# A buffer of its own for the convolution beside a recurrence, and scheduler priorities for the recurrence

## The chip, the cores and the metric

The kernel runs on one core of a Trainium2 chip. The metric is the device time of one execution in microseconds (us). Five engines work side by side, each through a queue of its own: TensorE (PE in the profile, with its weight loads as PEld), VectorE (DVE), ScalarE (ACT), GpSimd (POOL) and SyncE (SP), which here issues the transfers.

## The reference, cut to what matters

Two layers of a hybrid backbone over 768 tokens (256 of context, 512 latent), width 2048. In each layer one input projection feeds four groups of heads: a gating MLP, differential attention, a bidirectional recurrence (RWKV-7) and a short gated convolution. The recurrence and the convolution are the two that matter here:

```python
def rwkv_scan(r, k, v, decay, kk, a, s0):
    def step(S, inp):
        r_t, k_t, v_t, w_t, kk_t, a_t = inp
        sa = jnp.einsum('bhvk,bhk->bhv', S, -kk_t)
        S = (S * w_t[:, :, None, :] + sa[..., None] * (kk_t * a_t)[:, :, None, :]
             + v_t[..., None] * k_t[:, :, None, :])
        y = jnp.einsum('bhvk,bhk->bhv', S, r_t)
        return S, y

def short_conv(bg, cg, xin, w):
    z = cg * xin
    y = lax.conv_general_dilated(z, w[:, None, :].astype(z.dtype), window_strides=(1,),
                                 padding=[(CONV_W // 2, CONV_W // 2)], ...)
    return bg * y
```

The scan runs once forwards and once backwards over the context and then over the latent tokens; the two results are added, normalised by head and gated. All groups are gated, joined and sent through an output projection. The second layer needs no context outputs.

## The kernel before

**Main products.** A main product is a tile of 128 output features of a projection over all tokens (`mtile`). Each float32 weight tile is split into a high part `wh` (ACT, L276) and a low part `wl` (three of four on POOL, the rest on DVE, L277), and for each of the 16 blocks of 128 inputs three matmuls (L306) add high and low terms into PSUM: 48 matmuls of 512 columns for the latent tokens, and 48 of 256 for the context where it is wanted. The results rotate through three PSUM banks of the pool `mm`. A bank comes free when ACT or DVE has copied or used its result (`evac`, L331 and L333; `gate2`, L344 and L345).

**The recurrence.** It is cut into segments of 256 tokens: per layer 4 feature tiles (`ft`) times 3 parts times 2 directions, 24 segments, 48 in all. `rwkv_pipe` runs three of them in a pipeline: the chain of segment n, the inverse of segment n+1 and the preparation of segment n+2, then the outputs of n (`seg_y`) and the scores of n+2. The chain has four steps of 64 tokens. Each step is a matmul (L745), copies on DVE and ACT, a matmul (L748), copies again (L749, L750), a matmul (L753) and an update on DVE (L762), and the next step starts from that update; so each L748 belongs to one step, and four steps are a segment. When a feature tile's last segment is done, `rwkv_merge` normalises and gates its sum (L870 to L885) and stores it (L888); in the next tile's first segment this runs beside the chain.

**Where main products stand beside it.** The receptance, key and value tiles of a feature tile and its gates are projected while the segments before run; after the pipeline come convolution tiles (two in the first layer, all four in the second), each with four main products. After the recurrence the second layer goes on with attention: query, key and value products of a head, each copied to the tile `x`, rotated by a matmul with a table (L959), and so on.

**What sets the order.** The program is written for a scheduler that gives each engine a fixed order. Each instruction gets a running number as its priority, the lower first; among the instructions that are ready by its own model it takes the one with the lowest number. Work written in `with tc.high_priority():` has the number 0 and comes before everything: the splits of the weights, `evac`, `gate2` and the convolution's first product (L1105) are written so. Buffers carry tags: tiles of one tag share as many slots as `bufs` says, and a later tile waits until an earlier one is released. The convolution inside the recurrence (L1096 to L1106) takes its first tile from the tag `x` and its result from the tag `o`; these are also the tags of two accumulators of the feature tiles 0 and 2:

```python
st["yacc"] = rp.tile([128, PADW], F32, tag=("o", "yacc")[ft % 2], name=self.nm("yacc"))
st["bacc"] = rp.tile([128, PADW], F32, tag=("x", "bacc")[ft % 2], name=self.nm("bacc"))
```

Of the kernel before, what the change touches and what calls it, by code (L numbers as in the profile page):

```python
# [9 lines left out]
F32 = mybir.dt.float32  # L10
# [11 lines left out]
T = NCTX + NLAT  # L22
# [16 lines left out]
PADW = 774  # L39
# [64 lines left out]
class Kernel:  # L104
# [326 lines left out]
    def recurrence(self, l):  # L431
        nc, tc, ps = self.nc, self.tc, self.ps
        need = l < DEPTH - 1
        with tc.tile_pool(name=self.nm("rw"), bufs=1, reuse_waits="tile") as rp:
# [68 lines left out]
            for f in range((2, 4)[l]):  # L503
                self.conv(l, f)

    def rwkv_pipe(self, l):
        segs = []
        for ft in range(4):
            st = {}
            for i in range(3):  # L510
                for d in range(2):
                    segs.append(dict(l=l, ft=ft, d=d, i=i, st=st, last=(i == 2 and d == 1)))
        N = len(segs)
        merge = None
        for n in range(-2, N + 1):
            gens = []
            if 0 <= n < N:
                gens.append((self.seg_chain(segs[n]), 5))
            if 0 <= n + 1 < N:
                gens.append((self.seg_inverse(segs[n + 1]), 8))  # L520
            if n + 2 < N:
                gens.append((self.seg_pre(segs[n + 2]), 4))
            if merge is not None:
                gens.append((merge, 3))
                merge = None
            prog = [0.0] * len(gens)
            live = set(range(len(gens)))
            while live:
                g = min(live, key=lambda x: (prog[x], x))
                try:  # L530
                    next(gens[g][0])
                    prog[g] += 1.0 / gens[g][1]
                except StopIteration:
                    live.discard(g)
            if 0 <= n < N:
                self.seg_y(segs[n])
                if segs[n]["last"]:
                    merge = self.rwkv_merge(l, segs[n]["ft"], segs[n]["st"]["yacc"], segs[n]["st"]["bacc"])
            if n + 2 < N:
                self.seg_scores(segs[n + 2])  # L540
            yield n

    def seg_pre(self, s):
# [222 lines left out]
    def seg_y(self, s):  # L766
        l, ft, st, seg, want_y = (s[k] for k in ("l", "ft", "st", "seg", "want_y"))
        GM, SV, UV, AR = (s[k] for k in ("GM", "SV", "UV", "AR"))
        nc, rp, ps = self.nc, self.rp, self.ps
        V, A = nc.vector, nc.scalar  # L770
        if want_y:
            yp = ps.tile([128, 4, 2, 64], F32, tag="ps", name=self.nm("yp"))
            two = lambda t: t.rearrange("p a t -> p (a t)")
            for c in range(4):
                nc.tensor.matmul(out=yp[:, c], lhsT=two(UV[:, c]), rhs=GM[:, c, 1], start=True, stop=False)
                nc.tensor.matmul(out=yp[:, c], lhsT=two(SV[:, c]), rhs=AR[:, c, :, 1, :], start=False, stop=True)
            if "yacc" not in st:
                st["yacc"] = rp.tile([128, PADW], F32, tag=("o", "yacc")[ft % 2], name=self.nm("yacc"))
            ycol = st["yacc"][:, seg * SEG:(seg + 1) * SEG].rearrange("p (c t) -> p c t", c=4)
            for h in range(2):  # L780
                hs = slice(64 * h, 64 * h + 64)
                if st.get(("y", seg)):
                    V.tensor_tensor(out=ycol[hs], in0=yp[hs, :, h, :], in1=ycol[hs], op=ALU.add)
                else:
                    A.copy(out=ycol[hs], in_=yp[hs, :, h, :])
            st["y", seg] = True
# [302 lines left out]
    def conv(self, l, f):  # L1089
        nc, gp = self.nc, self.gp  # L1090
# [2 lines left out]
        cs = slice(0 if ctx else NCTX, T)  # L1093
        segs = ([(0, 0, NCTX, 2)] if ctx else []) + [(1, NCTX, NLAT, 260)]
        cw = self.P(l, "conv").rearrange("p (k f) -> p k f", k=3)
        x = gp.tile([128, T], F32, tag="x", name=self.nm("x"))  # L1096
        p = self.proj(l, 6336 + f * 128, ctx=ctx)
        self.evac(x[:, 0:NCTX], x[:, NCTX:T], p)
        zp = gp.tile([128, PADW], F32, tag="stg" if gp is self.rp else "cz", bufs=2, name=self.nm("zp"))
# [3 lines left out]
        for i, o0, n, po in segs:  # L1103
            with self.tc.high_priority():
                V.tensor_tensor(out=zp[:, po:po + n], in0=p[i][:, 0:n], in1=x[:, o0:o0 + n], op=ALU.mult)  # L1105
        o = gp.tile([128, T], F32, tag="o", name=self.nm("o"))  # L1106
        for i, o0, n, po in segs:
            s = slice(o0, o0 + n)
            A.activation(out=o[:, s], in_=zp[:, po:po + n], func=AF.Copy, scale=cw[:, 1, f:f + 1])
# [111 lines left out]

    def build(self):
        self.constants()
        for l in range(DEPTH):
            self.derived(l)
        self.od = [self.dp.tile([128, T], F32, name=f"od{k}") for k in range(KT)]
        self.xd = [[self.dp.tile([128, n], F32, name=f"x{v}_{k}") for k in range(KT)]
                   for v, n in ((0, NLAT), (1, NCTX))]
        self.lzd = [self.dp.tile([128, 2, PADW], F32, name=f"lzd{d}") for d in range(2)]
        self.rkvd = [[self.dp.tile([128, T], F32, name=f"rkvd{f}_{i}") for i in range(3)] for f in range(4)]  # L1230
        self.gd = [self.dp.tile([128, T], F32, name=f"gd{f}") for f in range(4)]
        self.nbuf = self.nxt = 0
        for l in range(DEPTH):
            self.first_phase(l)
            with self.tc.tile_pool(name=self.nm("os"), bufs=2, reuse_waits="tile") as self.osp:
                self.groups_phase(l)
                (self.out_mid if l < DEPTH - 1 else self.out_last)(l)
# [55 lines left out]
```

## Time and profile before

| what | value |
|---|---|
| median of 3 runs | 3751.13 us (3750.08 to 3751.83) |
| the profiled execution | 3740.13 us |
| its span, first to last instruction | 3738.3 us |
| PE busy | 3448.6 us, 92% |
| DVE busy | 2303.8 us, 62% |
| ACT busy | 1863.0 us, 50% |
| POOL busy | 1364.5 us, 36% |
| mean granted clock of PE | 0.959 |

The profile is of one execution. Its page gives busy times by engine, the span in 40 slices (each digit the busy share in tenths, PEclk the granted clock), and groups of instructions. Further views give busy times in stretches that one chooses, for all instructions or for one line of the program, and instructions in order of time. Matmuls overlap and their ends are modelled, so a busy PE is not PE at its peak, and a few matmul records can be missing. The first layer's recurrence lies at about 256 to 943 us of the span, the second's at about 2317 to 2965 us.

### The profile page before, as it was taken

The page shows a single profiled execution, that of the slowest core. Times are in us where ns is not written, and L with a number is a line of the kernel's source. Part 1 is how long each engine was busy: PE and PEld are TensorE (multiplying, and loading weights), DVE is VectorE, ACT ScalarE, POOL GpSimd, SP SyncE. Part 2 cuts the span into 40 slices and gives each one's busy share as a digit, 9 for nine tenths or more (in the row PEclk, how much of TensorE's full clock was granted, in tenths as well). Part 3 has the DMA queues.
Part 4 walks back from the last instruction along what each step waited for, and adds up shares of the span by engine and source line. Part 5 has one row for each costly group of instructions (what it writes and reads, how often), then busy time and mean ns, then how long its engine had stood idle before and what let it go on. Part 6 is the DMA issues. An engine that isn't in the chain of part 4 may idle for free. (4 is left out here: it accounts for less than half of the span.)

```text
span 3738.3 us, 61946 instructions
## 1 busy us (share of the span) xinstructions
PE 3448.6 (92%) x22388; PEld 2811.2 (75%) x22388; DVE 2303.8 (62%) x4659; ACT 1863.0 (50%) x4131; POOL 1364.5 (36%) x1729
## 2 busy tenths in 40 slices
PE   7999999989999999999897899999778999999998
PEld 2477777767877888888676777777566787788798
DVE  5856777777386546463878734767667526643354
ACT  4466666766244344223324435767666524544454
POOL 2244444534222222222444433545334332322343
PEclk9999999989999999999999999999668999999999
DMA  8432222211343313344655433122011244423565
GB/s 306 183 116 65 59 66 67 60 48 38 104 130 96 112 51 95 112 139 134 201 156 184 123 115 89 56 69 60 28 29 46 60 133 132 139 71 85 166 188 179
DMA packets 239747, 400.90 MB, mean 107 GB/s; under 512 B 25936, under 2 KB 95568, under 8 KB 235344
## 3 DMA queue, kind: packets, MB, share of 16 engines
q1 hardware_dynamic: 232528, 386.45, 34.3%
q10 hardware_dynamic: 6912, 10.49, 0.8%
q8 instruction: 176, 2.88, 0.3%
q14 instruction: 131, 1.07, 0.1%
HBM read 363.28 MB, written 33.56 MB: 106 GB/s over the span
## 5 line engine op out<-in xcount | busy, mean ns | idle before, releaser
L306 PE MATMUL p<-h,wh 128*128 128x512 f32 (+3 forms) x8576 | 2160.1, 349 | 34.5 <-ACT y L1160 10.7
L306 PEld LDWEIGHTS p<-h,wh 128*128 128x128 f32 (+1 forms) x8576 | 1415.4, 190 | 236.1 <-ACT h L276 15.8
L306 PE MATMUL p<-h,wl 128*128 128x512 f32 (+2 forms) x4288 | 1344.5, 350 | 46.1 <-DVE wl L277 28.9
L277 POOL TENSOR_TENSOR wl<-wr,wh 128x512 fp32r<-128x512 f32 (+1 forms) x535 | 768.4, 1439 | 1501.7 <-ACT wh L276 1317.8
L276 ACT CAST wh<-wr 128x512 fp32r<-128x512 f32 (+1 forms) x756 | 465.8, 617 | 974.1 <-PE p L306 772.2
L306 PEld LDWEIGHTS p<-h,wl 128*128 128x128 f32 (+1 forms) x4288 | 748.4, 190 | 147.7 <-DVE wl L277 35.8
L222 DVE SCALAR_TENSOR_TENSOR acc<-gw,sil,acc 128x512 f32<-128x512 f32 (+1 forms) x636 | 458.5, 778 | 27.4 <-DMA gw<-in_w_mod 25.1
L277 DVE TENSOR_TENSOR wl<-wr,wh 128x512 fp32r<-128x512 f32 (+1 forms) x221 | 160.9, 728 | 218.6 <-ACT wh L276 216.8
L804 PEld LDWEIGHTS <-ib 128*128 128x128 f16 x2304 | 133.2, 103 | 138.1 <-issue 70.0
L839 ACT CAST ib<-xa 64x256 f16<-64x256 f32 x480 | 176.2, 367 | 18.0 <-PE xa L809 12.2
L829 DVE TENSOR_TENSOR T<-inv,c 128x256 f16<-128x256 f32 x240 | 98.9, 412 | 34.5 <-PE inv L804 31.4
L1001 DVE TENSOR_REDUCE sm<-s 128x1 f32<-128x256 f32 (+1 forms) x144 | 74.8, 538 | 73.5 <-PE s L999 72.3
L741 POOL TENSOR_SCALAR sp<-SV,pcs 64x64 f32<-64x64 f32 x160 | 80.8, 509 | 105.5 <-DVE SV L762 81.0
L652 POOL TENSOR_TENSOR bk<-t_tw,kr 64x256 f32<-64x256 f32 x96 | 92.9, 968 | 36.1 <-DVE kr L636 32.4
L745 PE MATMUL ch<-SV,GM 128*128 128x128 f32 x384 | 89.5, 317 | 17.5 <-DVE SV L762 10.1
L1008 ACT ACTIVATE e<-s,sm 128x256 f32<-128x256 f32 (+1 forms) x144 | 80.9, 569 | 41.6 <-DVE sm L1005 33.3
L706 PE MATMUL g<-AR,BK 128*128 128x256 f32 (+1 forms) x384 | 96.7, 391 | 3.9 <-DVE BK L658 1.9
L748 PE MATMUL ch<-zs,xb 128*128 128x64 f32 x384 | 81.3, 296 | 15.0 <-ACT zs L747 13.6
L748 PEld LDWEIGHTS ch<-zs,xb 128*128 128x128 f32 x384 | 65.7, 204 | 38.5 <-ACT zs L747 32.5
L753 PE MATMUL ch<-UV,BKT 128*128 128x128 f32 x352 | 85.6, 328 | 9.6 <-ACT UV L750 8.6
L762 DVE SCALAR_TENSOR_TENSOR SV<-ch,pcs,sp 64x64 f32<-64x64 f32 x256 | 72.1, 281 | 35.4 <-PE ch L753 28.2
L745 PEld LDWEIGHTS ch<-SV,GM 128*128 128x128 f32 x384 | 64.4, 204 | 37.6 <-issue 9.3
(270 smaller groups left out, 5022.0 us busy)
## 6 DMA issues: line engine op xcount, KB each, us to landing
wr<-in_w_in SPq DMA_DIRECT2D x484, 256.0 KB, 2.7
wr<-in_w_out SPq DMA_DIRECT2D x256, 256.0 KB, 2.9
gw<-in_w_mod SPq DMA_DIRECT2D x192, 256.0 KB, 3.0
gw<-in_w_mod SPq DMA_DIRECT2D x32, 1024.0 KB, 6.6
gw<-in_w_mod SPq DMA_DIRECT2D x128, 128.0 KB, 3.2
raw<-rkvd SPq DMA_DIRECT2D x96, 128.5 KB, 2.2
lz<-lzd SPq DMA_DIRECT2D x48, 256.0 KB, 3.1
os<-od SPq DMA_DIRECT2D x32, 256.0 KB, 3.2
```

The lines of the kernel that those rows point to most:

```text
L222: self.nc.vector.scalar_tensor_tensor(out=acc, in0=w, scalar=s, in1=acc, op0=ALU.mult, op1=ALU.add)
L276: self.nc.scalar.copy(out=hi, in_=raw)
L277: eng.tensor_tensor(out=lo, in0=raw, in1=hi, op=ALU.subtract)
L306: nc.tensor.matmul(out=p[0:w, 0:n], lhsT=a[:, kk, :], rhs=x[b][k], start=(first and kk == 0 and i == 0), stop=(last and kk == 3 and i == 2))
L652: G.tensor_tensor(out=bk[hs, :, h, :], in0=c4(an)[hs], in1=kn[hs], op=ALU.mult)
L706: nc.tensor.matmul(out=g[:, c], lhsT=bkc(c2 + c), rhs=AR[:, c2 + c, :, 0:nk, :], start=True, stop=True)
L745: nc.tensor.matmul(out=chp[:, 0:128], lhsT=two(GM[:, c, 0]), rhs=two(SV[:, c]), start=True, stop=True)
L748: nc.tensor.matmul(out=chp[:, 128:192], lhsT=XT32[:, c, :], rhs=zs, start=True, stop=True)
L753: nc.tensor.matmul(out=chp[:, 192:320], lhsT=BKT[:, c, :], rhs=two(UV[:, c]), start=True, stop=True)
L804: nc.tensor.matmul(out=out[:, c, :], lhsT=lhsT[:, c, :], rhs=rhs(c), **kw(c))
L829: V.tensor_tensor(out=T1, in0=p1, in1=bt(self.lm(d, j)), op=ALU.mult)
L839: A.copy(out=half(XT, h), in_=aXT[hs])
```

## The change

Three things change. The accumulator `yacc` always takes a tag of its own, so the tag `o` is free while the pipeline runs. The convolution, when it runs inside the recurrence, uses one tile under the tag `o` both for its first copy and for its result, and none under `x`. And all that the pipeline issues (preparation, inverse, chain, merge, outputs, scores) goes through a new helper `ranked`, which gives it priority numbers that start 20000 below the running number at the pipeline's start and count up from there. The running number is set to 100000 after the constants, so that this stays above 0. What has the number 0 keeps it. The weight splits, transfers and products themselves are the same, instruction for instruction.

```diff
+    def ranked(self, fn, *args):
+
+        tc = self.tc
+        with tc.high_priority(offset=tc.cur_priority - self.rank):
+            try:
+                return fn(*args)
+            finally:
+                self.rank = tc.cur_priority
+
     def rwkv_pipe(self, l):
+        self.rank = self.tc.cur_priority - 20000
         segs = []
...
-                    next(gens[g][0])
+                    self.ranked(next, gens[g][0])
...
-                self.seg_y(segs[n])
+                self.ranked(self.seg_y, segs[n])
...
-                self.seg_scores(segs[n + 2])
+                self.ranked(self.seg_scores, segs[n + 2])
...
-                st["yacc"] = rp.tile([128, PADW], F32, tag=("o", "yacc")[ft % 2], name=self.nm("yacc"))
+                st["yacc"] = rp.tile([128, PADW], F32, tag="yacc", name=self.nm("yacc"))
...
-        x = gp.tile([128, T], F32, tag="x", name=self.nm("x"))
+        own = gp is self.rp
+        x = gp.tile([128, PADW if own else T], F32, tag="o" if own else "x", name=self.nm("x"))
...
-        o = gp.tile([128, T], F32, tag="o", name=self.nm("o"))
+        o = x if own else gp.tile([128, T], F32, tag="o", name=self.nm("o"))
...
         self.constants()
+        self.tc.cur_priority = 100000
```

Lines move by 10 to 12 numbers: L745, L748 and L753 become L755, L758 and L763, L870 and L876 become L880 and L886, L882 becomes L892. L306, L276, L277, L331 and L333 keep theirs.

The first place is PE's queue in the second layer, in the first chain step of the backward first segment of the third feature tile (`ch` is the chain's product, `p` a main product, `g`, `bt`, `lw` and `la` belong to the preparation of a later segment). Before:

```order
L706 MATMUL g_28786<-AR_22698,BK_28715 128x256 x2
L706 MATMUL g_28791<-AR_22698,BK_28715 128x256 x2
L745 MATMUL ch_28807<-SV_28442,GM_28445 128x128
L713 MATMUL bt_28796<-cst,BK_28715 128x128 x4
L603 MATMUL lw_28941<-lz_28860,wlh_27917 128x256
L604 MATMUL lw_28941<-lz_28860,wlo_27918 128x256
L605 MATMUL la_28942<-lz_28860,wlh_27917 128x256
L748 MATMUL ch_28807<-zs_28808,xb_22704 128x64
```

And now:

```order
L755 MATMUL ch_28805<-SV_28440,GM_28443 128x128
L306 MATMUL p_32756<-h_21008,wh_32759 128x512
L716 MATMUL g_28784<-AR_22696,BK_28713 128x256 x2
L716 MATMUL g_28789<-AR_22696,BK_28713 128x256 x2
L758 MATMUL ch_28805<-zs_28806,xb_22702 128x64
L306 MATMUL p_32756<-h_21007,wl_32760 128x512
L723 MATMUL bt_28794<-cst,BK_28713 128x128 x4
L306 MATMUL p_32756<-h_21014,wh_32759 128x512
L306 MATMUL p_32756<-h_21015,wh_32759 128x512
```

Matmuls of a convolution product now stand between the recurrence's; before there was none in this segment.

The second place is PE's queue just behind the second layer's last outputs (`yp`), where the last merge begins (`mp` and `vp` are its means). Before:

```order
L776 MATMUL yp_32178<-AR_22698,SV_31885 128x128
L306 MATMUL p_32760<-h_21065,wl_32800 128x512
L306 MATMUL p_32760<-h_21072,wh_32799 128x512
L306 MATMUL p_32760<-h_21073,wh_32799 128x512
L306 MATMUL p_32760<-h_21072,wl_32800 128x512
L306 MATMUL p_32760<-h_21079,wh_32799 128x512
L870 MATMUL mp_32189<-yacc_31555,cst 128x256
L306 MATMUL p_32760<-h_21080,wh_32799 128x512
```

And now, where `p_33751` is the first attention head's value product:

```order
L786 MATMUL yp_32176<-AR_22696,SV_31883 128x128
L880 MATMUL mp_32187<-yacc_31553,cst 128x256
L886 MATMUL vp_32192<-gn_32190,cst 128x256
L880 MATMUL mp_32202<-yacc_31553,cst 128x256
L886 MATMUL vp_32207<-gn_32205,cst 128x256
L306 MATMUL p_33751<-h_21000,wh_33755 128x512
```

The main products that surrounded the merge have moved ahead of it.

The third place is ACT's queue at the same point (`gn` and `yacc` belong to the merge, `x` is a copy out of a main product's bank). Before, with a convolution product's copy in the last row:

```order
L882 ACTIVATE yacc_31555<-yacc_31555,par_82 128x256
L276 CAST wh_32896<-wr_32894 128x512
L874 ACTIVATE gn_32207<-yacc_31555 128x256
L877 ACT_TABLE_LOAD
L877 ACTIVATE gn_32207<-vp_32209,eps 128x256
L276 CAST wh_32920<-wr_32918 128x512
L882 ACTIVATE yacc_31555<-yacc_31555,par_82 128x256
L276 CAST wh_32938<-wr_32936 128x512
L276 CAST wh_32956<-wr_32954 128x512
L333 COPY x_32838<-p_32839 128x512
```

And now, with the first query product's copy in the last row:

```order
L892 ACTIVATE yacc_31553<-yacc_31553,par_82 128x256
L884 ACTIVATE gn_32205<-yacc_31553 128x256
L887 ACTIVATE gn_32205<-vp_32207,eps 128x256
L892 ACTIVATE yacc_31553<-yacc_31553,par_82 128x256
L333 COPY x_33594<-p_33521 128x512
```

The splits of the next weights no longer stand between the merge's steps, and the copy that frees the query's bank follows directly behind the merge.

## Rows read from the trace of the kernel before

**Rows 1.** From the page: PE's busy time, then PE and its clock in 40 slices.
```profile
PE 3448.6 (92%) x22388; PEld 2811.2 (75%) x22388; DVE 2303.8 (62%) x4659; ACT 1863.0 (50%) x4131; POOL 1364.5 (36%) x1729
...
PE   7999999989999999999897899999778999999998
...
PEclk9999999989999999999999999999668999999999
```
**Rows 2.** Busy times by stretch: from:to, length, engines with instructions, clock, DMA share, GB/s.
```profile
core 0: us, PE busy (x) PEld busy (x) DVE busy (x) ACT busy (x) POOL busy (x), PEclk, DMA share, GB/s
...
2600.00:2700.00 100.00, 75.26 (x557) 60.25 (x557) 65.14 (x162) 63.13 (x162) 32.59 (x72) 0.64 0.10 30
```
**Rows 3.** The same view by segment, nine of 2338.6 to 2588.8: one, and the sum.
```profile
2468.00:2504.90 36.90, 34.56 (x268) 27.28 (x266) 26.13 (x59) 24.79 (x59) 16.16 (x25) 1.00 0.22 66
...
sum 250.20, PE 237.51 PEld 187.64 DVE 183.64 ACT 178.28 POOL 123.71; mean PE 26.39 PEld 20.85 DVE 20.40 ACT 19.81 POOL 13.75
```
**Rows 4.** The same for the next nine, 2588.8 to 2846.7: one, and the sum.
```profile
2616.40:2641.20 24.80, 18.75 (x157) 15.84 (x157) 14.66 (x38) 14.51 (x38) 7.50 (x18) 0.66 0.09 27
...
sum 257.90, PE 194.13 PEld 156.58 DVE 174.99 ACT 163.45 POOL 91.28; mean PE 21.57 PEld 17.40 DVE 19.44 ACT 18.16 POOL 10.14
```
**Rows 5.** Line L306 alone (main products: PE, PEld, clock, DMA) in three stretches.
```profile
2985.00:3065.00 80.00, 80.00 (x355) 66.24 (x354) 1.00 0.38 107
2588.80:2846.70 257.90, 6.03 (x14) 2.51 (x14) 0.68 0.10 29
2338.60:2588.80 250.20, 144.63 (x552) 86.90 (x551) 1.00 0.23 65
```
**Rows 6.** Busy times of two segments of the first layer, columns as in rows 2.
```profile
786.90:823.50 36.60, 26.87 (x184) 20.48 (x183) 25.43 (x55) 19.31 (x49) 10.85 (x20) 0.67 0.09 26
...
306.90:352.60 45.70, 44.88 (x344) 37.22 (x343) 23.33 (x55) 23.97 (x60) 19.93 (x32) 1.00 0.21 59
```
**Rows 7.** Instructions on tile x, 2300 to 3100: count, ns least/median/most, first and last start.
```profile
L333 ACT COPY x<-p x6: 577/582/591, 2838.7 to 3089.8; 128x512 f32<-128x512 f32 x6
L1105 DVE TENSOR_TENSOR zp<-p,x x4: 692/692/693, 2839.6 to 3039.0; 128x512 f32<-128x512 f32 x4
```
**Rows 8.** In order of time, the second layer's last chain copy and merge: start, length.
```profile
2964.89 0.21 ACT L750 COPY UV<-ch 64x64 f32<-64x64 f32 x1 [0.78 <-DVE UV L749]
...
2967.24 0.86 DVE L783 TENSOR_TENSOR yacc<-yp,yacc 64x256 f32<-64x256 f32 x2 [2.38 <-PE yp L776]
...
2971.93 1.75 DVE L878 RECIPROCAL gn<-gn 128x256 f32<-128x256 f32 x1 [0.18 <-ACT gn L877]
...
2984.28 0.33 SPq L888 DMA_DIRECT2D od<-yacc  x1
```
**Rows 9.** Instructions on tile yacc, 786 to 830, columns as in rows 7.
```profile
L879 DVE TENSOR_TENSOR yacc<-yacc,gn x3: 412/425/425, 793.5 to 824.1; 128x256 f32<-128x256 f32 x3
L882 ACT ACTIVATE yacc<-yacc,par x3: 600/602/602, 794.4 to 824.5; 128x256 f32<-128x256 f32 x3
L884 POOL TENSOR_TENSOR yacc<-yacc,bacc x3: 720/724/732, 795.1 to 825.3; 128x256 f32<-128x256 f32 x3
L885 DVE SCALAR_TENSOR_TENSOR yacc<-yacc,sgs x3: 424/426/426, 795.9 to 826.1; 128x256 f32<-128x256 f32 x3
```
**Rows 10.** In order of time, the first query's rotation, first and last step: start, length.
```profile
3072.60 1.12 PE L959 MATMUL rot<-x,rot 128*128 128x512 f32 x2
...
3077.81 1.40 DVE L971 TENSOR_TENSOR q<-x,q 64x512 fp32r<-64x512 f32 x2
```
**Rows 11.** Transfers by line: the rotation's larger table, its size, us to landing.
```profile
cs<-in_rope SPq DMA_DIRECT2D x2, 512.0 KB, 4.3
```
**Rows 12.** PE in order of time after a hole before 2004.2: start, length.
```profile
2004.20 0.80 PE L306 MATMUL p<-h,wh 128*128 128x256 f32 x2 [10.75 <-ACT y L1160]
...
2006.93 0.47 PE L306 MATMUL p<-h,wh 128*128 128x256 f32 x2
...
2008.43 0.40 PE L306 MATMUL p<-h,wh 128*128 128x256 f32 x2
```

## The prediction, made before the changed kernel ran

> **What bounds the kernel now.** I read the page first. TensorE (PE) is busy for 92% of the span, so only the few slices where it is not can give anything; in the slices of the second layer's recurrence its digit falls to 7 and the granted clock to 6 and 8 tenths [rows 1]. The next view is the busy time by stretches: from 2600 to 2700 us PE is busy 75% at a mean granted clock of 0.64, that is mostly at the lower of its two levels, 1.2 instead of 2.4 GHz [rows 2]. Then I cut the recurrence at its segments (the times are those of the first L748 matmul of each) and set nine consecutive segments that have main products beside them against the nine that follow and have almost none. The first nine last 250.2 us, with PE busy 237.5 [rows 3]; the second nine 257.9 us, busy 194.1 [rows 4]. The main products (L306) have 552 records in the first stretch, at clock 1.00, and 14 in the second, at 0.68 [rows 5]. So a segment takes about as long with products beside it as without: alone it is bound by the latency of its own chain through four engines, and what PE could have done meanwhile is lost. Why nothing fills it: the fused convolution tile's first copy out of PSUM and its product run from 2838.7 and 2839.6 us on, at the end of the empty stretch [rows 7]. Its buffers carry the tags x and o, which the third feature tile's two accumulators hold until that tile is merged; finished products sit in the three PSUM banks and stop the rest.
>
> **The change part by part.** No instruction is added or removed: each engine has the same count in both programs. What moves is their order, and outside the two recurrences and the entry to the second layer's attention PE's order is the same. The accumulator moves to its own buffer and the convolution uses one tile under the freed tag, so its products are no longer held. A main matmul of 512 columns costs 80.00 us over 355 records, 0.2254 us, in a stretch with nothing else [rows 5]; a few records may be missing, so this is an upper value.
>
> Step 1, what leaves the end. Behind the last chain matmul of the second layer, the new order has main columns worth 526 such matmuls fewer: 8 convolution products of 48, 22 of a ninth, the first query product (48) and the first key product (48 wide and 48 half as wide, 72). That stretch is bound by PE (80.00 busy of 80.00 [rows 5]), so 526 x 0.2254 = 118.6 us go.
>
> Step 2, what the recurrence pays. The nine empty segments get columns worth 508 matmuls instead of 10. The nine full ones before them carry 452 in 250.2 us [rows 3]. With 56 more, 250.2 + 56 x 0.2254 = 262.8. The empty nine also contain two segments that open a feature tile and merge the last one, the full nine one: that one takes 36.9 us against (250.2 - 36.9)/8 = 26.7 [rows 3]; its 26 extra matmuls explain 5.8 of the 10.2, so I add 4.4 and get 267.2. Against 257.9 [rows 4] this is +9.3. The other 28 of the 526 go into other segments: 28 x 0.2254 = +6.3. Net of steps 1 and 2: 118.6 - 9.3 - 6.3 = 103 us. A second way: idle time falls from 257.9 - 194.1 = 63.8 to 250.2 - 237.5 = 12.7 us, 51 less; and the recurrence's own PE time falls from some 190 us at clock 0.68 to 237.5 - 452 x 0.2254 + 4.4 = 140, 50 less. 101 us, so the two agree.
>
> Step 3, the first layer has one such hole: the segment at 786.9 us is 36.6 long, busy 26.9, at 0.67, while the one at 306.9 took 45.7 with PE busy 44.9, since main products went ahead of the chain there [rows 6]. In the new order the first gets 69 matmuls' worth in place of 19 and the second 51 in place of 126. By columns: 50 x 0.2254 = 11 us; by idle time (9.7 to some 1.5) and half of about 16 us at the low clock: 16. I take 13.
>
> Step 4, the ranking. It puts recurrence instructions ahead of main ones wherever both are ready. The splits of weights, the copies out of PSUM and the convolution's first product stay ahead of it (as before, at the top priority). The order shows nearly the same spacing as before: between a chain's consecutive matmuls stand 14 matmuls of other work in the median at each of the three places, against 13, 12 and 14. So I cost it at nothing for full segments; the cover is PE's own queue of products. On SP the loads for the segments now stand earlier between the weight loads; the DMA share in the full nine is 0.23 [rows 5], so there is room. If that cover failed, the price is in the slower rival.
>
> Step 5, a new wait. In the old order conv products surround the last merge; in the new one they are used up. PE's queue there holds only four merge matmuls, then the first value product, whose bank must be freed by the copy of the query product, and this copy stands on ACT behind both halves of the merge. I walk that path with durations of the old trace. Last chain copy at 2964.89, output sums from 2967.24 for 0.86 [rows 8], then mean, square, variance and root to the reciprocal's start at 2971.93, 1.75 long [rows 8]; multiply 0.43, ACT 0.60, POOL 0.72, DVE 0.43 [rows 9] bring 2975.9; the second half's reciprocal, multiply and ACT step take 1.75 + 0.43 + 0.60, then the copy 0.58 [rows 7]: 2979.3. PE has done its outputs by 2967.2 and has some 2.7 us of merge matmuls, so it stands about 9.4 us. Then the rotation's tables load, issued behind the merge's store at about 2980; the larger lands in 4.3 us [rows 11]. PE has seven products (1.6 us) until it wants the smaller, which I put at 2983.5: +2.6. The key product's banks wait for the query's rotation, 3072.60 to 3079.2 in the old trace [rows 10], against 4.5 us of products: +2. In all 14 us. After the old trace's hole of 10.75 us a pair of matmuls took 0.80 us first, 0.47 at 2006.93 and 0.40 later [rows 12]: some 3 us at the low clock, 1.5 us more. I take 16; 9 if only the merge shows, 25 if the merge's steps are held up as in the old trace, where it ended at 2984.28 [rows 8].
>
> **Sum:** 103 + 13 - 16 = 100 us. The profiled execution took 3740.1, so 3640 in its terms. The median of the runs is 3751.1, 0.3% above; in its terms 3651.
>
> **The port.** In the full nine POOL works 123.7 us and DVE 183.6 [rows 3], in the empty nine 91.3 and 175.0 [rows 4]. So 32.4 us of POOL work come beside the chain, and DVE's own rise of 8.6 us includes the splits that it takes itself. The Trainium skill, page "SBUF — State Buffer", section "Who interferes with whom", says that VectorE and GpSimd share a pair of ports which one instruction locks for its whole length while the other stands. By that rule the moved splits could delay the chain by up to their whole length. The rows bear this out little, since the full nine are no longer than the empty ones; it is a rival below.
>
> **The rivals.**
> - *The ranking also shortens the waits in full segments.* PE idles 12.7 us in nine [rows 3], at that rate some 68 us in all 48. If a chain that always comes first shortens this by a third, 23 us more go: 3628.
> - *The entry to attention costs far more.* If neither the merge (2964.9 to 2984.3, 19.4 us [rows 8]) nor the table's load (4.3 [rows 11]) nor the rotations of query and key (6.6 each [rows 10]) have cover, it is 37 us instead of 16: 3672. Against it: the value product does cover part.
> - *POOL's splits hold up the chain.* If all 32.4 us of them lengthen it: 3683.
> - *Slower:* PE takes its queue strictly in order. If the ranked matmuls stand one step too early, PE waits at each for DVE or ACT, where before a product lay between. From 2.1 us a segment over 48 segments the 100 us are gone; at 3 us, 144 lost, the time is 3795. For it: what idle time PE has in full segments is of just this kind. Against it: the spacing above, and that nine full segments idle only 12.7 us [rows 3] with a chain that is already taken first most of the time.
> - *The change doesn't do what it says:* the products stand in the gaps but their banks are still not freed, because a convolution tile's one buffer waits for its store. PE would then stand inside the segments: about 3751. A tile lasts some four segments, 105 us, against a 2 us store, so this is unlikely.
>
> **How the numbers follow.** Forecast 0.69; shorter waits 0.10; costly entry 0.10; port 0.05; no effect 0.02; slower 0.04. About 0.2% is what a measurement here can tell from no change, 7.5 us; so faster 0.94, same 0.02, slower 0.04. The bounds of the known terms are 104 + 16 - 9 = 111 and 101 + 11 - 25 = 87, that is 3640 to 3664; the range reaches to the entry's and the port's rivals above and the shorter waits below: 3622 to 3684.
>
> **What would show it.** Right: main products (L306) some 500 strong in the second layer's segments 11 to 19, clock 1.00 there, these segments 29 to 30 us long on average, the recurrence about 10 to 15 us longer, the stretch behind it some 118 us shorter; a PE hole near 10 us just after the last chain, ended by the copy of the query product. Wrong: segments beyond 32 us with PE idle 4 us or more in each, a hole above 30 us, or a low clock among the products.

## The result, and the profile after

The changed kernel takes 3651.05 us (median of 4 runs, 3648.28 to 3661.35) against 3750.61 (4 runs) of the kernel before on the same chip. The ratio is 0.9744, 95% interval 0.9721 to 0.9768: 99.6 us faster. Its profiled execution took 3652.25 us, 1.75 more than its span.

The page, answering to [rows 1]: PE is busy for 46.8 us less, although it runs the same instructions, and the low digits of the clock (6 and 8 tenths) in the second recurrence are gone.

```profile
PE 3401.8 (93%) x22388; PEld 2757.2 (76%) x22388; DVE 2300.6 (63%) x4659; ACT 1857.7 (51%) x4131; POOL 1359.1 (37%) x1729
...
PE   6999999999999999999888899999999988999998
...
PEclk9999999999999999999989999999999999999999
```

Busy times by stretch (from:to, length, engines with instructions, clock, DMA share, GB/s). The first row answers to [rows 2]; the next two are a full segment and the sum of the nine full ones, as in [rows 3]; then one segment and the sum of the nine that were empty, as in [rows 4]; then line L306 alone there, as in [rows 5]; then the two segments of the first layer, the later one first in [rows 6].

```profile
2600.00:2700.00 100.00, 95.18 (x732) 70.85 (x731) 75.54 (x163) 71.92 (x171) 50.70 (x84) 1.00 0.25 72
...
2472.70:2510.20 37.50, 34.85 (x266) 27.75 (x264) 28.94 (x63) 26.01 (x63) 16.61 (x30) 1.00 0.26 76
...
sum 249.40, PE 235.21 PEld 186.72 DVE 183.46 ACT 178.39 POOL 125.51; mean PE 26.13 PEld 20.75 DVE 20.38 ACT 19.82 POOL 13.95
...
2622.60:2647.10 24.50, 23.43 (x202) 17.85 (x202) 15.48 (x39) 17.07 (x43) 11.57 (x23) 1.00 0.25 71
...
sum 265.80, PE 253.11 PEld 191.01 DVE 200.05 ACT 190.53 POOL 136.83; mean PE 28.12 PEld 21.22 DVE 22.23 ACT 21.17 POOL 15.20
...
2593.30:2859.10 265.80, 161.81 (x512) 86.97 (x512) 1.00 0.25 72
...
312.00:339.10 27.10, 26.26 (x231) 21.39 (x229) 21.40 (x56) 19.05 (x53) 13.61 (x28) 1.00 0.20 60
778.40:815.20 36.80, 33.74 (x263) 27.59 (x263) 28.47 (x56) 21.77 (x54) 15.96 (x23) 0.95 0.20 55
```

The nine segments now hold 512 main matmuls at clock 1.00, where there were 14 at 0.68. They last 265.8 us instead of 257.9, and PE idles 12.7 us in them instead of 63.8. Instructions on the tile x between 2300 and 3100 us (count, ns least/median/most, first and last start) show the release that [rows 7] showed at 2838.7:

```profile
L333 ACT COPY x<-p x9: 564/588/593, 2520.6 to 3093.2; 128x512 f32<-128x512 f32 x9
...
L1116 DVE TENSOR_TENSOR zp<-p,x x4: 690/692/693, 2547.5 to 2855.3; 128x512 f32<-128x512 f32 x4
```

The first convolution tile's copy runs at 2520.6 us, and the four products (L1116) are spread over the recurrence, none behind it.

What PE waited for from the last chain on (total us, times, longest), the new wait of step 5:

```profile
PE s L1007 <- ACT e L1018: 6.2, 1, 6.2
PE vp L886 <- ACT gn L884: 4.8, 2, 3.8
PE p L306 <- ACT x L333: 3.9, 1, 3.9
PE p L306 <- ACT x L331: 2.8, 1, 2.8
PE rot L969 <- DMA rot<-in_rot: 2.5, 1, 2.5
PE mp L880 <- DVE yacc L793: 0.9, 1, 0.9
```

And the same place in order of time (start, length), answering to [rows 8]:

```profile
2974.41 0.21 ACT L760 COPY UV<-ch 64x64 f32<-64x64 f32 x1 [0.77 <-DVE UV L759]
...
2981.11 1.75 DVE L888 RECIPROCAL gn<-gn 128x256 f32<-128x256 f32 x1 [0.18 <-ACT gn L887]
...
2984.32 1.22 PE L886 MATMUL vp<-gn,cst 128*128 128x256 f32 x2 [3.85 <-ACT gn L884]
...
2988.83 0.56 ACT L333 COPY x<-p 128x512 f32<-128x512 f32 x1
...
2989.45 1.22 PE L306 MATMUL p<-h,wh 128*128 128x512 f32 x2 [3.91 <-ACT x L333]
...
2995.32 2.07 PE L969 MATMUL rot<-x,rot 128*128 128x512 f32 x2 [2.52 <-DMA rot<-in_rot]
```

The value product waits for the copy of the query product, which stands on ACT behind both halves of the merge. The second half's square (L884) stands on ACT behind the first half's scaling (L892), which itself waits for DVE's reciprocal and product; so PE's matmul for the second half (L886) waits 3.85 us in between. The granted clock falls there and again at 3030:

```profile
2980.00:2990.00 10.00, 2.24 (x6) 1.07 (x5) 5.45 (x7) 3.51 (x7) 1.45 (x2) 0.72 0.04 13
2990.00:3000.00 10.00, 7.48 (x16) 4.71 (x15) 1.57 (x3) 0.44 (x1) 1.28 (x1) 0.50 0.73 239
...
3030.00:3040.00 10.00, 3.79 (x15) 2.83 (x14) 8.63 (x15) 2.95 (x7) 0.56 (x1) 0.78 0.84 276
```

### The profile page after: what moved, and what is told of

Read it like the earlier page. It is cut to its first block, busy times and chain, and to the rows that moved or that the text cites. A ratio compares the mean times of both kernels' runs of the same rounds, so it can differ in the third digit from the quotient of the medians.

```text
span 3650.5 us, 61924 instructions
## 1 busy us (share of the span) xinstructions
PE 3401.8 (93%) x22388; PEld 2757.2 (76%) x22388; DVE 2300.6 (63%) x4659; ACT 1857.7 (51%) x4131; POOL 1359.1 (37%) x1729
## 5 line engine op out<-in xcount | busy, mean ns | idle before, releaser
L306 PE MATMUL p<-h,wh 128*128 128x512 f32 (+3 forms) x8576 | 2190.1, 351 | 37.5 <-ACT y L1171 10.5
L306 PEld LDWEIGHTS p<-h,wh 128*128 128x128 f32 (+1 forms) x8576 | 1417.2, 191 | 236.0 <-ACT h L276 17.3
L306 PE MATMUL p<-h,wl 128*128 128x512 f32 (+2 forms) x4288 | 1357.5, 352 | 45.3 <-DVE wl L277 27.2
L277 POOL TENSOR_TENSOR wl<-wr,wh 128x512 fp32r<-128x512 f32 (+1 forms) x535 | 761.5, 1425 | 1456.1 <-ACT wh L276 1298.2
L276 ACT CAST wh<-wr 128x512 fp32r<-128x512 f32 (+1 forms) x756 | 464.7, 616 | 893.1 <-PE p L306 667.4
L306 PEld LDWEIGHTS p<-h,wl 128*128 128x128 f32 (+1 forms) x4288 | 753.3, 191 | 146.2 <-DVE wl L277 33.7
L277 DVE TENSOR_TENSOR wl<-wr,wh 128x512 fp32r<-128x512 f32 (+1 forms) x221 | 162.5, 735 | 216.3 <-ACT wh L276 213.2
L814 PEld LDWEIGHTS <-ib 128*128 128x128 f16 x2304 | 117.9, 98 | 128.2 <-issue 72.8
L839 DVE TENSOR_TENSOR T<-inv,c 128x256 f16<-128x256 f32 x240 | 98.7, 411 | 25.4 <-PE inv L814 22.4
L845 ACT CAST X<-xa 128x256 f16<-128x256 f32 x192 | 71.4, 372 | 42.1 <-PE xa L819 39.5
L755 PE MATMUL ch<-SV,GM 128*128 128x128 f32 x384 | 82.0, 295 | 9.0 <-POOL GM L871 3.8
L656 DVE TENSOR_TENSOR AR<-kr,Pt 64x512 f32<-64x512 f32 (+1 forms) x96 | 83.8, 873 | 4.2 <-ACT Pt L631 2.2
L644 DVE RECIPROCAL t_sq<-t_sq 128x256 f32<-128x256 f32 x48 | 84.1, 1753 | 1.6
L205 PE MATMUL gr<-gw,sil 128*2 128x512 f32 x144 | 70.1, 625 | 15.6 <-DMA gw<-in_w_mod 15.6
## 6 DMA issues: line engine op xcount, KB each, us to landing
wr<-in_w_in SPq DMA_DIRECT2D x484, 256.0 KB, 2.7
wr<-in_w_out SPq DMA_DIRECT2D x256, 256.0 KB, 2.9
gw<-in_w_mod SPq DMA_DIRECT2D x192, 256.0 KB, 2.9
lz<-lzd SPq DMA_DIRECT2D x48, 256.0 KB, 3.1
os<-od SPq DMA_DIRECT2D x32, 256.0 KB, 3.3
```

What stands on the lines that cost most here:

```text
L276: self.nc.scalar.copy(out=hi, in_=raw)
L277: eng.tensor_tensor(out=lo, in0=raw, in1=hi, op=ALU.subtract)
L306: nc.tensor.matmul(out=p[0:w, 0:n], lhsT=a[:, kk, :], rhs=x[b][k], start=(first and kk == 0 and i == 0), stop=(last and kk == 3 and i == 2))
L644: V.reciprocal(out=sq, in_=sq)
L656: V.tensor_tensor(out=AR[hs, :, h, 0:nk, :], in0=kr[hs, :, 0:nk, :], in1=Pva[hs, :, 0:nk, :], op=ALU.mult)
L755: nc.tensor.matmul(out=chp[:, 0:128], lhsT=two(GM[:, c, 0]), rhs=two(SV[:, c]), start=True, stop=True)
```

## Experiments

For every kernel the span was cut at the first and the last matmul of the chain's second step in each layer. This table is worked out from those rows (us; each line is one profiled execution):

| kernel | to first chain | 1st recurrence | between | 2nd recurrence | behind | span |
|---|---|---|---|---|---|---|
| before | 256.0 | 687.1 | 1374.4 | 647.1 | 773.7 | 3738.3 |
| before_again | 256.2 | 689.1 | 1382.2 | 646.2 | 774.0 | 3747.7 |
| after | 263.6 | 672.6 | 1383.5 | 654.4 | 676.4 | 3650.5 |
| after_again | 263.3 | 673.2 | 1379.7 | 654.2 | 676.3 | 3646.7 |
| e1_buffers | 256.8 | 702.2 | 1349.3 | 648.8 | 682.5 | 3639.6 |
| e2_ranking | 265.4 | 663.1 | 1381.4 | 652.3 | 772.2 | 3734.4 |
| e3_two_convs | 265.4 | 672.3 | 1380.5 | 655.3 | 768.0 | 3741.5 |
| e4_early_copies | 263.7 | 673.0 | 1380.7 | 653.9 | 662.9 | 3634.2 |
| e4_again | 259.8 | 672.5 | 1382.1 | 655.4 | 665.2 | 3635.0 |
| e5_first_layer | 259.2 | 704.7 | 1352.9 | 646.6 | 770.2 | 3733.6 |
| e6_second_layer | 259.2 | 689.2 | 1371.4 | 648.6 | 677.4 | 3645.8 |
| e7_copies_unranked | 258.5 | 703.2 | 1343.6 | 648.6 | 673.5 | 3627.4 |
| e8_first_ranked | 266.6 | 670.8 | 1375.4 | 649.4 | 675.7 | 3637.9 |

**How far one execution can be read: before_again and after_again.**

> The kernel before, for a second profile of it. The parts of its span (start of the first chain, the two recurrences, the work between and behind them) were read from one execution, 256.0, 687.1, 1374.4, 647.1 and 773.7 us, whose span of 3738.3 us lies below the median of the runs. Theory A, the recurrences and the end repeat within 3 us and the parts that are bound by transfers (start, between) carry what differs from run to run: 687, 647 and 774 again, start and between up to 10 us longer. Theory B, what differs lies in the recurrences: they come out 5 to 10 us longer.

> The changed kernel once more, beside the others on the same chip. All theories: 3651 us within 5, PE standing some 16 us in all between the second layer's last chain step and the first head's scores.

The second profile of the kernel before took 3749.48 us. Both recurrences and the end repeat within 2 us, and 7.8 of the 9.4 us between the two spans lie in the work between the recurrences. The changed kernel again took 0.9745 of the kernel before (0.9725 to 0.9764; 3648.55 us). In after_again PE's waits behind the last chain are those of the changed kernel again (4.8, 3.9, 2.5 and 0.9 us, and 5.5 before the first scores, 17.6 in all where 16 were expected). The two profiles of e4, further down, differ by 3.9 us in the stretch ahead of the first chain and by up to 2.3 in the others. So the recurrences and the end can be compared from single profiles within some 2 us, the stretch ahead with some 4 us of doubt and the stretch between with some 8. The last three stretches of before_again, in the columns above:

```profile
945.30:2327.50 1382.20, 1290.76 (x7237) 1097.03 (x7237) 815.84 (x1445) 508.21 (x1000) 428.80 (x342) 0.97 0.41 123
2327.50:2973.70 646.20, 559.93 (x4510) 441.22 (x4509) 454.72 (x1103) 430.90 (x1094) 277.35 (x515) 0.88 0.17 48
2973.70:3747.70 774.00, 734.49 (x4246) 633.32 (x4245) 368.87 (x649) 343.27 (x646) 260.81 (x206) 0.98 0.45 136
```

And the last two of the changed kernel:

```profile
2319.70:2974.10 654.40, 620.74 (x5024) 479.46 (x5023) 482.26 (x1128) 457.89 (x1142) 325.33 (x553) 1.00 0.23 65
2974.10:3650.50 676.40, 623.11 (x3697) 538.24 (x3696) 345.25 (x625) 310.99 (x595) 217.39 (x167) 0.96 0.45 138
```

**Which half of the change does it: e1_buffers and e2_ranking.** e1 leaves the ranking out:

```diff
-                    self.ranked(next, gens[g][0])
+                    next(gens[g][0])
...
-                self.ranked(self.seg_y, segs[n])
+                self.seg_y(segs[n])
...
-                self.ranked(self.seg_scores, segs[n + 2])
+                self.seg_scores(segs[n + 2])
...
-        self.tc.cur_priority = 100000
```

> The buffers alone, without the ranking. Theory A (the gain is main products moved into empty segments, which the buffers allow; the ranking only redistributes among segments that are bound by PE): within 6 us of the changed kernel, 3645 to 3657; the first layer's segment of 45.7 us stays long, and both empty places are full. Rival B (the ranking is needed, since products that are overdue hold up the chain): the 19 us by which that one segment is too long are lost, 3670 or more.

e2 keeps the ranking and puts the old buffers back:

```diff
-                st["yacc"] = rp.tile([128, PADW], F32, tag="yacc", name=self.nm("yacc"))
+                st["yacc"] = rp.tile([128, PADW], F32, tag=("o", "yacc")[ft % 2], name=self.nm("yacc"))
...
-        own = gp is self.rp
-        x = gp.tile([128, PADW if own else T], F32, tag="o" if own else "x", name=self.nm("x"))
+        x = gp.tile([128, T], F32, tag="x", name=self.nm("x"))
...
-        o = x if own else gp.tile([128, T], F32, tag="o", name=self.nm("o"))
+        o = gp.tile([128, T], F32, tag="o", name=self.nm("o"))
```

> The ranking alone, the buffers as before. Theory A: the second layer's nine segments stay without main products (clock about 0.68 there), the entry to attention stays covered, and only the first layer's hole is filled, as the order shows: 3751 - 13 = 3738 us, 3733 to 3745. Rival B (the ranking does half of the work or more): 3700 or less. Rival C (ranked matmuls stand too early and PE waits for each): 3755 or more.

Measured: e1 0.9738 (0.9722 to 0.9754; 3647.72 us), as fast as the whole change; e2 0.9976 (0.9965 to 0.9988; 3735.96 us). The buffers alone carry the gain. As expected, e1 fills both empty places (PE is busy 35.5 of 37.4 us in the first layer's segment, 249.0 of 263.6 in the nine), and the first layer's long segment keeps its 45.7 us. e1 holds both changes of tags; which of the two is needed was not tried. The ranking alone is worth 9 us. In the second recurrence it costs some 5 us (652 to 655 us in every kernel that ranks it, 646 to 650 in every one that doesn't). In the first it fills the empty segment too (33.8 of 37.3 us busy in e2), by taking products away from the segment at 306.9 of [rows 6]; the buffers fill the same hole, so the two gains don't add.

**Which layer: e5_first_layer and e6_second_layer.** The kernel of e1 with the new tags in one layer only (shown for the first):

```diff
-                st["yacc"] = rp.tile([128, PADW], F32, tag="yacc", name=self.nm("yacc"))
+                st["yacc"] = rp.tile([128, PADW], F32, tag="yacc" if s["l"] == 0 else ("o", "yacc")[ft % 2], name=self.nm("yacc"))
...
-        own = gp is self.rp
+        own = gp is self.rp and l == 0
```

> The buffer change without the ranking, in the first layer's recurrence alone; the second layer's is as before. By the order some 110 matmuls' worth of main columns move from behind the first layer's recurrence into it, 59 of them into its one empty segment. Theory A, the earlier profile of the buffers in both layers holds for this half too: its second recurrence began 9 us earlier than before's, so 3736 us against 3745 of the kernel before (3732 to 3740). Theory B, the whole 13 us that the prediction took for the first layer: 3732. Theory C, this recurrence had no room to give, since all its segments but one were already full, and what is moved in lengthens it by as much: 3745.

> The buffer change without the ranking, in the second layer's recurrence alone; the first layer's is as before. Theory A, the two layers' gains add up: 97 us for both less 9 for the first leaves 88, so 3657 us against 3745 of the kernel before (3652 to 3662). Theory B, if the first layer gives the predicted 13: 3661. Theory C, if it gives nothing, all of the gain is here: 3648.

Measured: e5 0.9959 (0.9946 to 0.9971; 3731.23 us), 15 us, nearest to the predicted 13. e6 0.9751 (0.9736 to 0.9766; 3654.69 us), 92 us, within the bounds of its first theory. The two sum to 107 us where both together (e1) gave 97; with intervals of some 5 us on each of the three it stays open whether they add. How each layer gains differs. In e5 the recurrence becomes longer and the work behind it shorter by more:

```profile
259.20:963.90 704.70, 672.56 (x5556) 544.72 (x5556) 507.56 (x1166) 465.17 (x1168) 316.17 (x561) 0.99 0.20 59
963.90:2316.80 1352.90, 1261.93 (x7089) 1072.19 (x7089) 811.87 (x1441) 501.36 (x989) 423.05 (x337) 0.97 0.41 125
```

In e6 the second recurrence takes 472 more instructions of PE than before_again in 2.4 us more, and the end is 97 us shorter:

```profile
2319.80:2968.40 648.60, 615.01 (x4982) 471.76 (x4981) 480.63 (x1126) 456.19 (x1139) 320.09 (x550) 1.00 0.22 65
2968.40:3645.80 677.40, 631.15 (x3774) 547.42 (x3773) 347.77 (x626) 313.55 (x599) 222.68 (x170) 0.97 0.46 139
```

**Is it the fill: e3_two_convs.** The changed kernel with two of the second layer's four convolution tiles taken out of its recurrence; they run behind it, after the second and the fourth attention head:

```diff
-            for f in range((2, 4)[l]):
+            for f in range(2):
                 self.conv(l, f)
...
-            late = ({('a', 1): 2, ('a', 3): 3}, {})[l]
+            late = {('a', 1): 2, ('a', 3): 3}
```

> The changed kernel with two convolution tiles beside the second layer's recurrence in place of four; the other two run after the second and the fourth attention head, as in the first layer. By the order 384 matmuls' worth of columns go back behind the recurrence, and its segments from the 17th on are empty again. Theory A, a product that has no cover costs its columns, one that stands in a segment next to nothing: 384 x 0.2254 = 87 us more behind the recurrence, some 7 us less in it, so about 3728 us against 3649 of the changed kernel (3715 to 3738); the empty segments take 27 to 29 us on average at a clock near 0.68. Theory B, the second half of the recurrence gains as much from an empty queue as it loses, or attention covers the two tiles better: 3649 to 3690.

Measured: 0.999 (0.998 to 1.000; 3741.97 us), above the range expected (3715 to 3738). The fill is the cause, and its absence costs more than the 80 us expected: some 92 (0.999 against the changed kernel's 0.9745 of the kernel before). Of five segments that are empty again, the first, and the sum:

```profile
2796.60:2821.70 25.10, 18.91 (x144) 16.03 (x143) 13.99 (x35) 13.68 (x36) 7.20 (x17) 0.59 0.09 27
...
sum 141.80, PE 104.80 PEld 84.39 DVE 94.57 ACT 87.21 POOL 50.27; mean PE 20.96 PEld 16.88 DVE 18.91 ACT 17.44 POOL 10.05
```

The same five in the changed kernel, full, last 145.80 us:

```profile
sum 145.80, PE 138.74 PEld 104.71 DVE 109.19 ACT 103.26 POOL 76.29; mean PE 27.75 PEld 20.94 DVE 21.84 ACT 20.65 POOL 15.26
```

The fill costs 4 us in five segments, and the recurrence as a whole was not the expected 7 us shorter without it (655.3 against 654.4), while the end was 91.6 us longer instead of 87. So 384 matmuls' worth of columns were all but free in the segments.

**The hole at the entry: e4_early_copies.** The changed kernel, in which the first head's query and key products are copied out inside the recurrence, into its buffers, stored, and loaded back when attention begins:

```diff
             for f in range((2, 4)[l]):
                 self.conv(l, f)
+            for i in range(0 if need else 2):
+                p = self.proj(l, 1536 + 512 * i, ctx=i > 0)
+                t = rp.tile([128, PADW], F32, tag=("x", "o")[i], name=self.nm("qk"))
+                self.evac(t[:, 0:NCTX], t[:, NCTX:T], p)
+                lo = 0 if i else NCTX
+                nc.sync.dma_start(out=self.qkd[i][:, lo:T], in_=t[:, lo:T])
...
-            p = self.proj(l, c0 + h * 128, ctx=ctx)
-            x = tT("x")
-            self.evac(x[:, 0:NCTX], x[:, NCTX:T], p)
+            if need_ctx or h:
+                p = self.proj(l, c0 + h * 128, ctx=ctx)
+                x = tT("x")
+                self.evac(x[:, 0:NCTX], x[:, NCTX:T], p)
+            else:
+                x, lo = tT("x"), 0 if ctx else NCTX
+                nc.sync.dma_start(out=x[:, lo:T], in_=self.qkd[s == "k"][:, lo:T])
...
+        self.qkd = [self.dp.tile([128, T], F32, name=f"qkd{i}") for i in range(2)]
```

> The changed kernel, and the second layer's first query and key products are copied out of PSUM inside the recurrence, into its own buffers, go to DRAM and come back into attention's tile, so that their banks no longer wait for the last merge and the value product stands around the merge. Theory D (the hole is the merge on ACT ahead of the bank's release, 16 us with its low clock): 3651 - 14 = 3637 us, 3632 to 3642; no hole behind the last chain. Rival E (the wait only moves, to the rotation, which needs tables and copies loaded behind the merge's store): 3647 to 3655, with a hole of 10 us or more a little later.

Measured: 0.9712 (0.9698 to 0.9726; 3636.73 us), and once more as e4_again 0.9709 (0.9696 to 0.9723; 3635.94): 12 us faster than the changed kernel.

> The changed kernel with early copies once more, beside the two variants. It took 0.9712 of the kernel before (0.9698 to 0.9726); about 3637 us again.

In the 20 us behind the chain PE does not stop any more:

```profile
2972.60:2992.60 20.00, 20.00 (x114) 17.22 (x114) 9.56 (x11) 6.52 (x11) 5.27 (x5) 1.00 0.31 96
```

The same stretch of the changed kernel:

```profile
2975.40:2995.40 20.00, 7.81 (x28) 4.84 (x27) 6.90 (x10) 4.62 (x8) 1.45 (x2) 0.72 0.22 73
```

Some waits come back later: up to 3100 us PE stands 8.7 us for a copy out of a bank (2.8 in the changed kernel) and 4.7 us for the loads.

```profile
PE p L306 <- ACT x L331: 8.7, 1, 8.7
PE rot L979 <- DMA x<-qkd: 4.7, 2, 3.5
```

**Early copies with less ranking: e7_copies_unranked and e8_first_ranked.** e7 is e4 without the ranking; e8 ranks in the first layer alone:

```diff
         tc = self.tc
+        if not self.in_first:
+            return fn(*args)
         with tc.high_priority(offset=tc.cur_priority - self.rank):
...
         self.rank = self.tc.cur_priority - 20000
+        self.in_first = l == 0
```

> The buffers and the early copies without the ranking. Theory A, the ranking is worth nothing and the early copies are worth the 12 us that they gave with it: the buffers without ranking took 3648, so 3636 us (3631 to 3641). Theory B, the ranking is what lets the early copies pass the merge, and without it the hole at the entry comes back in part: 3642 to 3648. In its profile A wants the stretch behind the recurrence 13 us shorter than without the copies (about 665 to 670 us).

> The buffers and the early copies, with the ranking in the first layer's recurrence alone. In the profiles the ranking lengthened the second recurrence by some 5 us (654 against 649) and shortened the end by up to 6, and in the first layer shortened the recurrence by as much as start and the work between grew. Theory A, these are exchanges of order and come to nothing: 3636 us, as with the ranking in both (3632 to 3640). Theory B, the 5 us in the second recurrence are a price of the ranking there: 3631.

Measured: e7 0.9709 (0.9691 to 0.9727; 3631.65 us), e8 0.9711 (0.9698 to 0.9725; 3638.18 us). With e4 all three are equal: beside the buffers the ranking is worth nothing that intervals of 5 to 7 us could show. These versions beat both kernels, e7 with the lowest median. But e7's end is 673.5 us, not the 665 to 670 expected, and only 4 to 9 shorter than that of e6 and e1. The waits of e6 behind its chain show how much less there was to win: without the ranking the merge opens hardly any hole, since main products still stand around it.

```profile
PE p L306 <- ACT x L331: 5.9, 2, 3.0
PE s L1007 <- ACT e L1018: 4.7, 1, 4.7
PE rot L969 <- DMA rot<-in_rot: 1.2, 1, 1.2
...
PE p L306 <- ACT x L333: 0.8, 1, 0.8
```

A wait for the merge (vp) is among them with 0.2 us only. The ranking pulls the merge ahead of the last products (the second place of the change) and so opens the hole; in exchange it leaves fewer products for the end (3120 records of L306 against 3198 in e6, by columns 58 matmuls' worth, some 13 us). The two about cancel. By the ratios e7 beats e1 by 11 us; what the early copies still win there, without the hole, was not taken apart.

## Why the prediction was right, step by step

Forecast 3651, measured 3651.05; the mechanism is the one that was named, but that the number is met so closely is partly chance. In terms of two profiles each, the mean span falls from 3743.0 to 3648.6, by 94.4, and beside after_again the medians differ by 96.5; the forecast sum was 100. Three terms were off: the end by 5 and the first layer by 8 to the worse, the second recurrence by 8 to the better. Of the signs named, the filled segments (512 main matmuls, clock 1.00, 29.5 us on average) and the hole ended by the query's copy came out; the recurrence is only 7.6 us longer, not 10 to 15, the end is 97.5 us shorter, not 118, and a low clock did show among products, just behind the entry (0.50).

- **Steps 1 and 5, the end**: -118.6 and +16, so -102.6 predicted; 773.9 to 676.4, -97.5, measured. Against before_again PE is busy for 734.49 - 623.11 = 111.4 us less there and idles 13.8 us more. The sum of the idle time is what was predicted (14), its parts only partly: the merge 4.8 + 3.9 + 0.9 = 9.6 (predicted 9.4) and the rotation's table 2.5 (2.6) are where they were put. The 2 us for the first key's banks did not appear, and the 6.2 us before the first scores (L1007) and the 2.8 behind L331, in the second head, were not foreseen. The sum fits because old waits went too: up to 3100 us PE idles 22.4 us, where before_again idled 6.8 up to the same place (550.5 us from the end, 2973.7 to 3197.2), and the last 550.5 us hold 30.9 and 32.7. That the sum fits is luck. The mis-sized term is the low clock, 1.5 predicted: 118.6 - 111.4 leaves 7.2 us. In the two stretches at clock 0.50 (2984.3 to 3001.4 us and 3035.5 to 3042.4) PE works 14.3 us. A pair of matmuls took 0.80 us at the low clock and 0.40 at the full one in [rows 12], so half of that, some 7 us by this estimate, is the clock's; that is about all of it, and what is left may be the price per product, which was an upper value.
- **Step 2, the second recurrence**: +15.6 predicted, +7.6 measured (646.7 to 654.3). The nine segments came out nearly as worked out, 265.8 for 267.2. The 28 other matmuls' worth, +6.3, cost nothing visible, and most of them do not lie there: the recurrence has 514 more records of L306 (823 to 1337), 498 of them in the nine, and the end 550 fewer. Nor are the 7.6 us the products' alone: e6, without the ranking, takes in 472 more and is only 2.0 longer (648.6). So these 472 cost the recurrence about 2 us, far from the 15.6 forecast for all, and most of the 7.6 comes with the ranking, which step 4 put at nothing, and the 42 records that its order adds. PE's idle time in this recurrence falls from 86.3 to 33.7, 52.6 less (51 predicted).
- **Step 3, the first layer**: the segments moved as the order said (27.1 and 36.8 us, clock 0.95). The 13 us are borne out by the buffers in this layer alone (15, e5). In the changed kernel the recurrence gains 15.2, but 7.4 go ahead of the first chain, where the ranking puts more main products (L306 is busy 120.9 us there for 115.9); of the rest, some 4 us are within what that stretch differs by from profile to profile. With the work between, these three stretches gain 4.5, within the doubt of the stretch between.
- **Step 4, the ranking at nothing**: right as a sum (e1 against after_again, e7 against e4), though it moves some 30 us from one stretch to another and costs the second recurrence some 5. The rival that it shortens the waits falls: the nine full segments idle 249.40 - 235.21 = 14.2 us, before 12.7 [rows 3]. So does the slower rival, with 1.4 to 1.6 us idle in a segment of either kind.
- **The costly entry** fell: 118.6 - 97.5 = 21 us, not 37, for the 16 predicted.
- **The port** fell as a price and held as a mechanism. POOL works 136.8 us in the nine segments, 45.5 more than in [rows 4], and they last 7.9 longer. What lengthened shows in the groups by line, DVE in those nine segments (count, busy us, mean ns, idle before), of the kernel before

```profile
L762 DVE SCALAR_TENSOR_TENSOR SV<-ch,pcs,sp 64x64 f32<-64x64 f32 x48 | 13.5, 282 | 7.0 <-PE ch L753 5.5 <-POOL bk L652 0.7
...
L658 DVE TENSOR_TENSOR BK<-bk,t_L 128x512 f32<-128x512 f32 x9 | 6.1, 678 | 0.4 <-POOL bk L652 0.2
```

and of the changed kernel, the same two:

```profile
L772 DVE SCALAR_TENSOR_TENSOR SV<-ch,pcs,sp 64x64 f32<-64x64 f32 x48 | 13.4, 279 | 4.2 <-PE ch L763 3.2
L668 DVE TENSOR_TENSOR BK<-bk,t_L 128x512 f32<-128x512 f32 x9 | 9.6, 1063 | 2.0 <-POOL bk L662 1.3 <-ACT X L845 0.6
```

The product of the preparation (BK) takes 1063 ns on average instead of 678; the chain's update (SV) is unchanged. The average mixes two kinds: three of the nine take 1.67 to 1.84 us, the other six 0.69 to 0.75. In order of time, one of the three, and one that began before POOL's split (L277) did:

```profile
2697.86 1.62 POOL L277 TENSOR_TENSOR wl<-wr,wh 128x512 fp32r<-128x512 f32 x1
2698.36 1.67 DVE L668 TENSOR_TENSOR BK<-bk,t_L 128x512 f32<-128x512 f32 x1
...
2779.70 0.69 DVE L668 TENSOR_TENSOR BK<-bk,t_L 128x512 f32<-128x512 f32 x1 [0.64 <-ACT X L845]
2779.74 1.78 POOL L277 TENSOR_TENSOR wl<-wr,wh 128x512 fp32r<-128x512 f32 x1
```

At each of the three long ones a split had started just before (the split shown, 1.62 us long, had itself begun beside another such product, L656). Where BK started first it kept its 0.69 us, and the split took 1.78 instead of the usual 1.28. In e3's second recurrence from 2796.6 us on, with POOL's splits gone again (and the casts and products beside them), it takes 680:

```profile
L668 DVE TENSOR_TENSOR BK<-bk,t_L 128x512 f32<-128x512 f32 x5 | 3.4, 680 | 0.1
```

The Trainium skill, page "SBUF — State Buffer", section "Who interferes with whom", says that a VectorE instruction with two inputs in SBUF contends with a GpSimd instruction that reads SBUF. The rows agree: BK has two such inputs, while the chain's update reads its product from PSUM. What the rival missed is which instructions are held up: those of the preparation, two segments ahead, and not those on the chain.

## What to carry to other kernels

When a segment is bound by the latency of its own chain, look for what keeps independent products out of its gaps; here shared tags did, and with them freed 512 main matmuls cost some 8 us in nine segments and saved most of their price at the end. A change of order that empties the queue behind a phase opens holes at its boundary: walk the first products of the next phase and see whose buffer each waits for. Test an added priority by itself: here it was worth 9 us alone; beside the buffers it moved tens of microseconds between stretches and summed to nothing.

## What was not expected of the hardware

The recurrence's segments hardly become shorter when PE is theirs alone: five empty ones take 141.8 us at a clock of 0.59 to 0.72, the same five full ones 145.8 at 1.00. And the low clock outlasted the hole at the entry: after waits of 3.85, 3.91 and 2.52 us within 11 us, PE was busy 7.5 of the 10 us from 2990 on, all at 0.50. Whether full clock alone would shorten an empty segment was not tried.

A small price of the change shows in the first layer: with one slot for `yacc`, the next tile's accumulator waits for the merge's store. The store of one merge lands at 463.30 us, and ACT, idle for 0.9 us until then, starts its first copy into the next accumulator (L795) at 463.32; so again at 643.17 and 643.19. What this costs in time was not tried.
